# Sparse attention: the softmax of the compressed branch moved from ahead of the attention units to beside the scores of the first three

## The chip, the cores and the metric

The kernel runs on one core of a Trainium2 chip. The metric is the time of one execution of the whole program in device microseconds (us); the time before is the median of three runs. The program is a whole two-block network for 512 tokens (mixer with two kinds of attention, feed-forward layers, a second mixer, 32 experts); the change touches a stretch of some 30 us in the first mixer.

## The reference, cut to what matters

The sparse attention has three branches that share the queries: one over 31 compressed keys, one over selected blocks and one over a window. Each has a softmax of its own, and three gates weigh the results:

```python
s_c = jnp.einsum('btgrd,bjgd->bgrtj', q, k_cmp, ...) * scale
s_c = s_c - slopes[:, :, None, None] * dist_c
p_cmp = _masked_softmax(s_c, dist_c >= 0)
o_cmp = jnp.einsum('bgrtj,bjgd->btgrd', p_cmp.astype(v_cmp.dtype), v_cmp)
...
o = g[:, :, 0] * o_cmp + g[:, :, 1] * o_sel + g[:, :, 2] * o_win
```

With 512 tokens the 16 selected blocks and the window both hold every earlier token, so the second and third branch are full causal attention with a distance penalty. There are 8 heads in 2 groups; a head has 64 columns.

## The kernel before, in words

The stage is the function `nsa`. Its work has three parts.

**The compressed branch.** For each of the two groups, eight matmuls (L2111) give the scores of four heads against the compressed keys, transposed, in a PSUM tile of tag `sc`; ScalarE copies it to SBUF as `scT` (L2113). Then a loop over the four blocks of 128 tokens does the softmax: TensorE transposes the block of both groups back (L2119, two transposes, into `sc`), VectorE adds the mask (L2123), takes the maximum (L2124), subtracts it (L2125), multiplies by the slopes (L2126), ScalarE takes the exponential (L2127), VectorE sums (L2128), inverts (L2130), applies the gate (L2131, L2133) and scales (L2134), TensorE transposes the result `ec` (L2137, into a PSUM tile `pt`), ScalarE copies the high part to `PcTH` (L2138) and VectorE subtracts for the low part `PcTL` (L198, a helper's line). `PcT` is used first by the matmuls L2153 at the end of unit 1.

**The units.** `attend` runs 16 units, two branches for each of 8 heads. `att_scores` makes the scores of a unit in four row blocks of 128, 256, 384 and 512 keys (two matmuls L1973 each, of at least 256 columns, into `sc`); VectorE adds the penalty and takes the row maximum as it moves them to SBUF as `E` (L1975), and negates the maxima (`nm`, L1979). One step later `att_exp` takes the exponentials on ScalarE (L1987), inverts the sums (L1989), applies the gate (L1991) and scales `E` (L1996 on GpSimd and VectorE, L1994 on ScalarE). Another step later `att_av` transposes `E` (L2044), splits it into a high and a low part (L2050 on ScalarE, L198 on VectorE) and multiplies it with the values (L2053). So a unit is spread over three steps.

**The fill.** The matmuls of eight gate panels (L386, L389, tile `gm`) need nothing of this stage. `drip` hands them out in pieces of two, behind scores, transposes and output matmuls, at fixed rates (`FA`).

PSUM gives the tag `sc` two places; the compressed scores, their transposes and the scores of the units share them. The tag `pt` has three places. Before the change the tile `scT` lies in two of the three places of the tag `E3`, the 512-key block of a unit.

What each engine does next is an order that the framework fixes when the program is built: it takes instructions by the place where they are written, by what they depend on and by an internal estimate of times. An engine works off its list in that order, and a row that waits holds up all rows behind it. Weights come through SyncE's DMA queue, one panel of 512 KB at a time.

Of the kernel before, what the change touches and what calls it, by code (L numbers as in the profile page):

```python
# [8 lines left out]
F32 = mybir.dt.float32  # L9
# [7 lines left out]
T, D, P = 512, 1024, 128  # L17
NT = T // P
# [148 lines left out]
class Net:  # L167
# [1886 lines left out]
                          stop=u["last"] and j == NT - 1 and x is L, skip_group_check=True)  # L2054
            self.drip(last, self.rate)

    def attend(self, units, sp, pp, rate, lag=2):

        n = len(units)
        self.att_pad(sp)  # L2060
        self.rate = rate
        for t in range(n + lag):
            if t < n:
                u = units[t]
                if u.get("pre"):
                    u["pre"](u)
                self.att_scores(u, sp, pp)
            if 0 <= t - 1 < n:
                self.att_exp(units[t - 1], sp)
            if t >= lag:  # L2070
                u = units[t - lag]
                self.att_av(u, sp, pp)
                if u.get("post"):
                    u["post"](u)
        while self.pieces_:
            self.pieces_.pop(0)()
# [20 lines left out]
    def nsa(self, qst, KS, Vst, PcT, vcs, kcmp, gt, tb, oN, fill):  # L2097
        tc, V, S, PE = self.tc, self.V, self.S, self.PE
        with ExitStack() as st:
            sp = st.enter_context(tc.tile_pool(name="spn", bufs=1, reuse_waits="tile"))  # L2100
            self.at = st.enter_context(tc.tile_pool(name="spns", bufs=1, reuse_waits="tile"))
            pp = st.enter_context(tc.tile_pool(name="ppn", bufs=1, space=PSUM, reuse_waits="tile"))

            self.fill_start(fill, pp)
            tabc = tb["tabc"].rearrange("p (i j) -> p i j", i=NT)
            scT = []
            for g in range(2):
                ps = pp.tile([P, T], F32, name="sc", tag="sc", bufs=2)
                for x in range(2):
                    for j in range(4):  # L2110
                        last = PE.matmul(ps, lhsT=kcmp[x][:, g, 96 - 32 * j:224 - 32 * j], rhs=qst[:, 4 * g + j, :], start=x + j == 0, stop=x == 1 and j == 3)  # L2111
                scT.append(sp.tile([P, T], F32, name="scT", tag="E3", bufs=3))
                self.act = S.activation(scT[g], ps, AF.Copy)  # L2113
                self.drip(last, self.FA[1])
            for i in range(NT):
                tk = slice(i * P, (i + 1) * P)
                ps = pp.tile([P, 8, 32], F32, name="sc", tag="sc", bufs=2)
                for g in range(2):
                    last = PE.transpose(ps[:, 4 * g:4 * g + 4, :].rearrange("p a b -> p (a b)"), scT[g][:, tk], self.ident)  # L2119
                self.drip(last, self.FA[3])  # L2120
                e = sp.tile([P, 8, 32], F32, name="ec", tag="ec", bufs=2)
                m = self.at.tile([P, 8], F32, name="mc", tag="mc", bufs=2)
                V.tensor_tensor(e, ps, tabc[:, i, None, :].to_broadcast([P, 8, 32]), op=ALU.add)  # L2123
                V.tensor_reduce(m, e, axis=mybir.AxisListType.X, op=ALU.max)  # L2124
                V.tensor_tensor(e, e, m[:, :, None].to_broadcast([P, 8, 32]), op=ALU.subtract)  # L2125
                V.tensor_tensor(e, e, tb["slope"][:, :, None].to_broadcast([P, 8, 32]), op=ALU.mult)  # L2126
                S.activation(e, e, AF.Exp)  # L2127
                V.tensor_reduce(m, e, axis=mybir.AxisListType.X, op=ALU.add)  # L2128
                c = self.at.tile([P, 8], F32, name="ccc", tag="ccc", bufs=2)
                V.reciprocal(c, m)  # L2130
                V.tensor_tensor(c, c, gt[:, 0:8, i], op=ALU.mult)  # L2131
                if i == 0:
                    V.tensor_scalar(c, c, tb["valid"], None, op0=ALU.mult)  # L2133
                V.tensor_tensor(e, e, c[:, :, None].to_broadcast([P, 8, 32]), op=ALU.mult)  # L2134
                pt = pp.tile([P, 2, P], F32, name="pt", tag="pt", bufs=3)
                for g in range(2):
                    last = PE.transpose(pt[:, g, :], e[:, 4 * g:4 * g + 4, :].rearrange("p a b -> p (a b)"), self.ident)  # L2137
                self.act = S.activation(PcT[0][:, :, tk], pt, AF.Copy)  # L2138
                self.sub(PcT[1][:, :, tk], pt, PcT[0][:, :, tk])
                self.drip(last, self.FA[2])  # L2140
            units = []
            for h in range(8):
                g = h // 4
                cell = {}

                def newO(cell=cell):
                    cell["O"] = pp.tile([P, T], F32, name="O", tag="O", bufs=2)
                    return cell["O"]

                def post(u, h=h, g=g):  # L2150
                    r = slice((h % 4) * 32, (h % 4) * 32 + 32)
                    for x in range(2):
                        PE.matmul(u["O"], lhsT=vcs[r, g, :], rhs=PcT[x][r, g, :], start=False, stop=x == 1, skip_group_check=True)  # L2153
                    self.head_out(u["O"], oN, h, sp)

                for b in range(2):
                    units.append(dict(q=[qst[:, h, :]], k=KS[b][g], v=lambda j, b=b, g=g: Vst[:, j, 2 * b + g, :], tab=tb["tab"],
                                      scale=2.0 ** -(h + 1), gate=gt[:, 8 * (b + 1) + h, :], first=b == 0, last=False,
                                      O=None, newO=newO if b == 0 else (lambda cell=cell: cell["O"]), post=post if b else None))
            self.attend(units, sp, pp, self.FA[0])  # L2160


# [19 lines left out]
```

## Time and profile before

| | us |
|---|---|
| median of three runs | 1741.72 (1736.89 to 1745.83) |
| the profiled execution | 1744.53 |
| its span in the trace | 1742.7 |
| TensorE busy | 1636.6 (94%) |
| VectorE busy | 1246.2 (72%) |
| ScalarE busy | 934.2 (54%) |
| GpSimd busy | 380.8 (22%) |

The span is what the trace covers; 1.8 us of the profiled execution lie around it. The profiled execution is 2.8 us above the median. Busy shares are of the whole span, so the stretch of the change has to be read by itself: it lies from 92 us (first compressed scores) to 225.6 us (last output matmul of the stage).

### The profile page before, as it was taken

How to read it: one execution, taken by the hardware profiler on the slowest of the kernel's cores; microseconds unless marked ns; L12 is line 12 of the kernel's file. 1: busy time of each engine (PE TensorE's matmuls, PEld its weight loads, DVE VectorE, ACT ScalarE, POOL GpSimd, SP SyncE). 2: the span in 40 equal slices, each digit the busy share in tenths (PEclk: the TensorE clock that was granted, in tenths of full speed). 3: DMA queues.
4: the chain of work that ended last, by engine and by line, in shares of the span. 5: the costliest groups of instructions: out<-in, count | busy, mean ns of one | idle time of the engine just before them, and what ended most of it. 6: DMA issues, size and time to landing. Idle time of an engine off the chain costs nothing.

```text
span 1742.7 us, 24957 instructions
## 1 busy us (share of the span) xinstructions
PE 1636.6 (94%) x8980; PEld 1381.0 (79%) x8980; DVE 1246.2 (72%) x2281; ACT 934.2 (54%) x1588; POOL 380.8 (22%) x243
## 2 busy tenths in 40 slices
PE   8989999999999999999999999969999999989993
PEld 8868787877888888788769878758888788878882
DVE  5767857757787666533787875687888878897786
ACT  3457845664254444322554333346676667766763
POOL 3323401314144442000373221120100000101001
PEclk9989999999999999999999997969999999999997
DMA  5401213216333333322323212559999999999983
GB/s 153 108 25 38 43 55 68 60 37 226 128 109 97 97 97 97 114 92 70 116 84 98 79 43 67 208 176 340 381 387 402 374 400 406 405 363 402 391 345 109
DMA packets 214862, 317.55 MB, mean 182 GB/s; under 512 B 41997, under 2 KB 142524, under 8 KB 214735
## 3 DMA queue, kind: packets, MB, share of 16 engines
q1 hardware_dynamic: 209263, 303.91, 49.9%
q0 software_dynamic: 5472, 12.01, 1.9%
q8 instruction: 72, 1.18, 0.3%
q14 instruction: 55, 0.45, 0.1%
HBM read 308.06 MB, written 15.73 MB: 186 GB/s over the span
## 4 chain that ended last, share of the span: by engine, by line
PE 57%; DVE 8%; ACT 4%; DMA 3%; issue 3%; POOL 1%; DVEq 0%; SPq 0%; ACTq 0%; POOLq 0%
PE pA L205 13%; PE gate L1656 9%; PE pA L208 6%; PE up L1668 5%; PE dn L1702 5%; PE pA L810 4%; PE pA L809 4%; PE pA L811 4%; PE pA L958 2%; DVE wl L198 2%; ACT wh L1624 1%; DVE xL L198 1%; DMA raw<-in_w_up 1%; DMA raw<-in_w_down 1%; PE pB L278 1%
## 5 line engine op out<-in xcount | busy, mean ns | idle before, releaser
L198 DVE TENSOR_TENSOR wl<-wr,wh 128x1024 fp32r<-128x1024 f32 (+5 forms) x185 | 219.2, 1187 | 155.1 <-ACT wh L244 97.7
L241 POOL TENSOR_TENSOR wr<-wr,cols 128x1024 f32<-128x1024 f32 (+2 forms) x91 | 196.4, 2162 | 368.3 <-DMA wr<-in_w_in 135.4
L244 ACT ACTIVATE wh<-wr 128x1024 fp32r<-128x1024 f32 (+3 forms) x163 | 158.9, 980 | 193.0 <-PE pA L205 75.2
L1656 PEld LDWEIGHTS gate<-Xf,raw 128*128 128x128 f32 x2048 | 248.8, 191 | 11.2 <-ACT sil L1660 0.4
L198 DVE TENSOR_TENSOR wl<-raw,wh 128x1024 fp32r<-128x1024 f32 x172 | 207.0, 1227 | 54.3 <-ACT wh L1624 52.7
L1656 PE MATMUL gate<-Xf,raw 128*128 128x64 f32 x2048 | 243.3, 271 | 0.0
L205 PE MATMUL pA<-xL,wh 128*128 128x512 f32 (+1 forms) x544 | 193.6, 365 | 0.0
L205 PE MATMUL pA<-xH,wh 128*128 128x512 f32 (+1 forms) x544 | 193.3, 365 | 0.0
L1624 ACT ACTIVATE wh<-raw 128x1024 fp32r<-128x1024 f32 x172 | 175.1, 1051 | 12.2 <-PE dn L1702 6.5
L208 PE MATMUL pA<-xH,wl 128*128 128x512 f32 (+1 forms) x544 | 121.9, 365 | 0.0
L198 DVE TENSOR_TENSOR xL<-raw,xL 128x1024 fp32r<-128x1024 f32 x84 | 101.6, 1221 | 21.8 <-ACT xL L1624 20.5
L205 PEld LDWEIGHTS pA<-xL,wh 128*128 128x128 f32 x544 | 102.7, 189 | 16.7 <-issue 0.4
L205 PEld LDWEIGHTS pA<-xH,wh 128*128 128x128 f32 x544 | 102.5, 189 | 16.8 <-issue 0.4
L208 PEld LDWEIGHTS pA<-xH,wl 128*128 128x128 f32 x544 | 94.3, 189 | 16.0
L1624 ACT ACTIVATE xL<-raw 128x1024 fp32r<-128x1024 f32 x84 | 86.9, 1052 | 8.9 <-PE pC L1391 5.2
L1480 POOL DMA_INDIRECT Xr<-hnD,ix x16 | 23.7, 1482 | 248.9 <-issue 145.5
L1829 POOL DMA_INDIRECT yD<-yp,ix x14 | 23.4, 1673 | 212.7 <-DVE yp L1715 192.8
L810 PE MATMUL pA<-wh,actL 128*128 128x512 f32 x176 | 68.7, 390 | 0.0
L809 PE MATMUL pA<-wh,actH 128*128 128x512 f32 x176 | 68.5, 390 | 0.0
L811 PE MATMUL pA<-wl,actH 128*128 128x512 f32 x176 | 67.8, 390 | 0.0
L1702 PE MATMUL dn<-wl,hst 128*128 128x512 f32 x172 | 60.3, 414 | 3.9 <-DVE wl L198 3.2
L1996 POOL TENSOR_SCALAR E<-E,cc 128x128 f32<-128x128 f32 (+1 forms) x48 | 42.8, 901 | 91.1 <-DVE cc L1989 31.1
(691 smaller groups left out, 3799.8 us busy)
## 6 DMA issues: line engine op xcount, KB each, us to landing
raw<-in_w_gate SPq DMA_DIRECT2D x128, 512.0 KB
raw<-in_w_up SPq DMA_DIRECT2D x128, 512.0 KB
raw<-in_w_down SPq DMA_DIRECT2D x128, 512.0 KB
wr<-in_w_up SPq DMA_DIRECT2D x44, 512.0 KB
wr<-in_w_in SPq DMA_DIRECT2D x43, 512.0 KB
wr<-in_w_down SPq DMA_DIRECT2D x22, 512.0 KB
wr<-in_w_o SPq DMA_DIRECT2D x8, 512.0 KB
yD<-zero SPq DMA_DIRECT2D x8, 512.0 KB
```

The costliest lines, as they stand in the source:

```text
L198: return self.V.tensor_tensor(out, a, h.bitcast(F32), op=ALU.subtract)
L205: self.PE.matmul(ps, lhsT=ws(wh, k), rhs=xs(x, k), start=n == 0, stop=False)
L208: last = self.PE.matmul(ps, lhsT=ws(wl, k), rhs=xs(xh, k), start=False, stop=k == nk - 1)
L241: self.G.tensor_tensor(raw, raw, g[:, :, None].to_broadcast([P, nk, ncol]), op=ALU.mult)
L244: self.S.activation(H, raw, AF.Copy)
L809: self.PE.matmul(ps, lhsT=xs(0, a, i), rhs=H[:, k, :], start=a == 0, stop=False)
L810: self.PE.matmul(ps, lhsT=xs(1, a, i), rhs=H[:, k, :], start=False, stop=False)
L811: self.PE.matmul(ps, lhsT=xs(0, a, i), rhs=L[:, k, :], start=False, stop=a == nk - 1)
L1624: self.S.activation(H, raw, AF.Copy)
L1656: self.PE.matmul(ps[:, f, :], lhsT=raw[:, k, f * P:(f + 1) * P], rhs=u["Xf"](2 * p + k), start=p + k + f == 0, stop=p == 3 and k == 1, ski ...
L1668: self.PE.matmul(u[tag], lhsT=u["Xg"](2 * p + k), rhs=W[:, k, :], start=p + k == 0 and W is HL[0], stop=p == 3 and k == 1 and W is HL[1])
L1702: PE.matmul(u["dn"][hf], lhsT=u["hs"][:, p, :], rhs=W[:, 0, c], start=p == 0 and W is HL[0], stop=p == 3 and W is HL[1])
```

## The change

The body of the loop over the four blocks becomes a local function `compressed(i)`. `attend` gets a new argument, a table of functions for a step: after it has written the scores of unit t it calls the functions of step t. `nsa` hands it block 0 for step 0, blocks 1 and 2 for step 1 and block 3 for step 2. The tile `scT` gets a tag of its own with two places (4 KB more in each partition). Nothing is computed differently. In the changed file the lines of the block lie four further down (L2119 is L2123, L2137 is L2141).

```diff
-    def attend(self, units, sp, pp, rate, lag=2):
+    def attend(self, units, sp, pp, rate, beside={}, lag=2):
...
                 self.att_scores(u, sp, pp)
+            for f in beside.get(t, ()):
+                f()
             if 0 <= t - 1 < n:
                 self.att_exp(units[t - 1], sp)
...
-                scT.append(sp.tile([P, T], F32, name="scT", tag="E3", bufs=3))
+                scT.append(sp.tile([P, T], F32, name="scT", tag="scT", bufs=2))
...
-            for i in range(NT):
+
+            def compressed(i):
+
...
-            self.attend(units, sp, pp, self.FA[0])
+
+            self.attend(units, sp, pp, self.FA[0], {0: [lambda: compressed(0)], 1: [lambda: compressed(1), lambda: compressed(2)], 2: [lambda: compressed(3)]})
```

On TensorE, from the last gate pieces that go with the compressed scores, the order before has all eight transposes back and then the transposes of the first block's result:

```order
L386 MATMUL gm<-xL,wh 128x512
L2119 MATMUL sc<-ident,scT 128x128 x8
L2137 MATMUL pt<-ident,ec 128x128 x2
L386 MATMUL gm<-xH,wh 128x512
L386 MATMUL gm<-xL,wh 128x512
L2137 MATMUL pt<-ident,ec 128x128 x2
```

In the changed kernel the scores of unit 0 stand at that place, with two pairs of gate matmuls among them, and only then the first block's transposes:

```order
L1973 MATMUL sc<-KL_108,qst 128x256
L386 MATMUL gm<-xH,wh 128x512
L386 MATMUL gm<-xL,wh 128x512
L1973 MATMUL sc<-KH_107,qst 128x384
L1973 MATMUL sc<-KL_108,qst 128x384
L386 MATMUL gm<-xH,wh 128x512
L386 MATMUL gm<-xL,wh 128x512
L1973 MATMUL sc<-KH_107,qst 128x512
L1973 MATMUL sc<-KL_108,qst 128x512
L2123 MATMUL sc<-ident,scT 128x128 x2
```

The transposes back of the last block now follow the scores of unit 2. A little later on TensorE, in the changed kernel, the transposes of the third and fourth block's result stand like this, with the first scores of unit 3 ahead of them:

```order
L1973 MATMUL sc<-KL_112,qst 128x256
L2141 MATMUL pt<-ident,ec 128x128 x2
L386 MATMUL gm<-xH,wh 128x512
L386 MATMUL gm<-xL,wh 128x512
L386 MATMUL gm<-xH,wh 128x512
L386 MATMUL gm<-xL,wh 128x512
L386 MATMUL gm<-xH,wh 128x512
L386 MATMUL gm<-xL,wh 128x512
L386 MATMUL gm<-xH,wh 128x512
L386 MATMUL gm<-xL,wh 128x512
L2141 MATMUL pt<-ident,ec 128x128 x2
```

Eight gate matmuls have come between the two pairs of transposes; before, six L389 and the scores of unit 2 followed the fourth pair.

On VectorE the changed kernel's list of this stretch ends like this (PcTL is the last product of a block; the scores behind it are those of unit 3):

```order
L2134 RECIPROCAL ccc<-mc 128x8
L2135 TENSOR_TENSOR ccc<-ccc,gt 128x8
L198 TENSOR_TENSOR PcTL<-pt,PcTH 128x2x128
L2138 TENSOR_TENSOR ec<-ec,ccc 128x256
L198 TENSOR_TENSOR PcTL<-pt,PcTH 128x2x128
L1975 ISA E,mx<-sc,ta 128x128
L1975 ISA mx 128x1
L1975 ISA E,mx<-sc,ta 128x256
L1975 ISA mx 128x1
L198 TENSOR_TENSOR PTl<-pt,PTh 128x512
```

The scores of unit 3 stand behind the fourth block's PcTL; before, all of the four PcTL stood ahead of the last three scores of unit 2.

Because the order of the whole program comes out of one pass, other places change too, with the same instructions in another order. SyncE's queue of expert weights is one:

```order
-L1383 DMA hnD<-hnt 128x512 x4
-L1611 DMA raw<-in_w_down 128x1024
-L1383 DMA hnD<-hnt 128x512
+L1383 DMA hnD<-hnt 128x512 x5
+L1611 DMA raw<-in_w_down 128x1024
 L1611 DMA raw<-in_w_up 128x1024
 L1611 DMA raw<-in_w_gate 128x1024
```

Here one expert load moved behind a store; further down some 220 rows of loads stand in another order.

## Rows read from the trace of the kernel before

**Rows 1.** The page: span, busy time of TensorE, DMA share by slice.
```profile
span 1742.7 us, 24957 instructions
...
PE 1636.6 (94%) x8980; PEld 1381.0 (79%) x8980; DVE 1246.2 (72%) x2281; ACT 934.2 (54%) x1588; POOL 380.8 (22%) x243
...
DMA  5401213216333333322323212559999999999983
```

**Rows 2.** Busy time of each engine by stretch of the stage.
```profile
core 0: us, PE busy (x) PEld busy (x) DVE busy (x) ACT busy (x) POOL busy (x), PEclk, DMA share, GB/s
...
100.29:105.69 5.40, 0.00 (x1) 0.00 (x0) 5.19 (x14) 0.84 (x2) 2.15 (x1) 0.71 0.01 2
105.69:109.40 3.71, 3.67 (x12) 2.88 (x12) 2.87 (x10) 0.77 (x2) 0.00 (x0) 0.51 0.00 0
109.40:112.90 3.50, 2.35 (x8) 1.19 (x8) 3.50 (x18) 0.84 (x2) 0.00 (x0) 0.98 0.00 0
112.90:116.10 3.20, 3.19 (x10) 2.71 (x10) 1.77 (x10) 2.57 (x9) 0.00 (x0) 0.50 0.04 8
116.10:120.70 4.60, 3.29 (x18) 2.30 (x17) 4.60 (x16) 4.04 (x12) 2.87 (x2) 0.99 0.00 0
...
126.83:225.60 98.77, 96.28 (x543) 79.54 (x541) 77.73 (x230) 76.91 (x205) 34.92 (x34) 1.00 0.19 40
```

**Rows 3.** TensorE's waits from 92 to 230 us: total, times, longest.
```profile
PE pt L2137 <- DVE ec L2134: 5.4, 1, 5.4
PE sc L1973 <- DVE mx L1975: 1.9, 4, 0.7
...
PE pt L2044 <- POOL E L1996: 1.2, 1, 1.2
```

**Rows 4.** TensorE's timeline: start us, length us, engine, line, operation, [idle before <-releaser].
```profile
105.69 0.69 PE L2137 MATMUL pt<-ident,ec 128*128 128x128 f32 x2 [5.40 <-DVE ec L2134]
...
126.36 0.40 PE L386 MATMUL gm<-xH,wh 128*128 128x512 f32 x1
126.60 0.39 PE L386 MATMUL gm<-xL,wh 128*128 128x512 f32 x1
```

**Rows 5.** VectorE's timeline in the softmax of the first two blocks.
```profile
99.04 0.76 DVE L2123 TENSOR_TENSOR ec<-sc,ta 128x256 f32<-128x256 f32 x2 [1.90 <-PE sc L2119]
99.71 0.73 DVE L2124 TENSOR_REDUCE mc<-ec 128x8 f32<-128x256 f32 x2
...
101.03 2.45 DVE L2126 TENSOR_TENSOR ec<-ec,ta 128x256 f32<-128x256 f32 x2
...
104.31 0.32 DVE L2130 RECIPROCAL ccc<-mc 128x8 f32<-128x8 f32 x2
104.54 0.29 DVE L2131 TENSOR_TENSOR ccc<-ccc,gt 128x8 f32<-128x8 f32 x2
```

**Rows 6.** VectorE's timeline in the work of the units.
```profile
117.79 0.48 DVE L1996 TENSOR_SCALAR E<-E,cc 128x512 f32<-128x512 f32 x1
118.27 0.42 DVE L1975 CUSTOM_DVE_ANT_0 E<-sc,ta 128x256 f32<-128x256 f32 x1
...
118.62 1.22 DVE L198 TENSOR_TENSOR wl<-wr,wh 128x1024 fp32r<-128x1024 f32 x1
119.76 0.55 DVE L1975 CUSTOM_DVE_ANT_0 E<-sc,ta 128x384 f32<-128x384 f32 x1
...
120.23 0.69 DVE L1975 CUSTOM_DVE_ANT_0 E<-sc,ta 128x512 f32<-128x512 f32 x1
...
120.84 0.18 DVE L1989 RECIPROCAL cc<-sm 128x4 f32<-128x4 f32 x1
```

**Rows 7.** GpSimd's timeline at 101 us.
```profile
101.06 2.15 POOL L241 TENSOR_TENSOR wr<-wr,cols 128x1024 f32<-128x1024 f32 x1 [12.42 <-DMA wr<-in_w_in]
```

**Rows 8.** The expert stage: busy time as in rows 2, SyncE's longest wait.
```profile
1300.00:1400.00 100.00, 95.75 (x623) 81.59 (x621) 79.78 (x119) 67.83 (x101) 7.92 (x6) 1.00 1.00 391
...
SPq L1611 <- PE gate L1656: 127.9, 86, 4.6
```

## The prediction, as it was put on record

> **What bounds the kernel now.** I read the page first: TensorE is busy for 94% of the span, and the DMA engines are full only in the last third [rows 1]. So the time goes through TensorE up to the experts, and through DMA and TensorE together from there. Then I read the stage of the change in stretches [rows 2]. From 126.83 to 225.6 us TensorE is busy for 96.3 of 98.8 us: the steady run of the units is bounded by it, and no engine near it waits long. Ahead of that it is not. From 100.29 to 105.69 TensorE does nothing while VectorE is busy for 5.2 of 5.4 us: TensorE has made the transposes back of all four blocks' scores, and its next row, the transposes of the first block's result, waits for the scaling L2134 [rows 3, 4]. After that gap the granted clock is 0.51 for 3.7 us, the lower of the two levels (1.2 instead of 2.4 GHz); it rises, TensorE then waits for VectorE to empty the score tiles (four waits, 1.9 us) and the clock is at 0.50 again from 112.9 to 116.1 [rows 2, 3]. What is lost ahead of the steady run is thus 5.4 + 1.9 + 1.2 us of waits and half of 3.7 + 3.2 us at the low clock, 3.5 us: **12 us is the ceiling** of what this change can give back in its own stretch.
>
> The chain there is VectorE's. So the question is how much VectorE has to do until the steady run can start, and how long it waits itself.
>
> **The change part by part.** Nothing is removed or added: the same 8 + 8 transposes, 37 softmax operations on VectorE, 4 exponentials. They move to other places, and I follow one mark that both orders have: the pair of gate matmuls L386 behind the first two output matmuls of unit 0. Before, its second matmul starts at 126.60 [rows 4]. Up to the mark both orders have the same gate matmuls, the same scores of units 0 to 3, the same transposes; the order before also has two matmuls of unit 4, 256 columns each, together 0.23 us (half of the 0.24 us between two 512-column starts [rows 4], twice). What lies behind the mark is bounded by TensorE in both (the last line of [rows 2]), so what the mark wins is kept to the end of the stage, and all later work is moved by it.
>
> VectorE's list up to the mark, with times from start to start. A block of the softmax has seven passes over 256 columns, 0.335 us each (two L2123 from 99.04 to 99.71), and two small ones of about 0.12 us (two L2130 in 0.23) [rows 5]: 2.6 us, four blocks 10.4 us. A unit has four score passes, 0.35 us for 256, 0.47 for 384, 0.61 for 512 columns [rows 6], and 0.21 for 128 by the same step (an estimate from these three); with the scaling of E, 0.48, and three small ones, 0.4 in all, 2.5 us; three units 7.6 us. One split of a gate panel (wl) is 1.14 us [rows 6]. Together **19.1 us** from 99.0, when the first scores are there as the first transposes were: 118.1. Then two scores of unit 3 (0.56) and the first PTl (0.61, as 512 columns): 119.3, and TensorE needs one output matmul and one gate matmul more: the mark at 119.8. That is VectorE without a wait, 6.8 us earlier than now, 6.6 us net of unit 4's matmuls.
>
> It will wait in three places, as I find by going through the new order row by row with these durations. First, the scores of unit 0 go through two PSUM places by turns, each filled by TensorE only when VectorE has emptied it: 0.8 us until the first L2123 of the new order (VectorE's mask). Second, at the end: the third block's transposes wait for VectorE until about 116.9, and the fourth block's stand behind eight gate matmuls (8 x 0.23 = 1.84 us); VectorE finishes its other rows at about 118.8, and its next row, the last PcTL, can start at 119.9: 1.1 us, in which the scores of unit 3, long made, lie behind the waiting row. Third, the transposes of unit 0's E come only behind that pair, and its PTl 0.9 us later than VectorE could take it. So the mark comes at 119.8 + 2.8 = 122.6, 4.0 us earlier; **3.8 us net**.
>
> Two costs the trace of before bounds only. The clock: in my walk TensorE does about 0.8 us of work between 105.6 and 109.1, less than the 2.35 us busy of 109.4 to 112.9, behind which the clock was 0.50 [rows 2]; and it waits some 3.3 us from 113.7 to 117.0, behind which I expect what the 5.4 us gap brought. At the low clock the eight L389 and later the eight L386 take 1.8 us more each; of the first some 1.0 us reaches VectorE (it delays the 512-column scores of unit 2, which VectorE takes next), of the second all. Between 0 and 2.8 us; I take 2.0, since both patterns are nearer to rows that were followed by the low clock than to 116.1 to 120.7, which was not. The port: one L2126 of the first two took 2.1 us instead of 0.34 while GpSimd worked on a gate panel at 101.06 [rows 5, 7]. The panel comes at the same time, and in the new order VectorE reads PSUM in most of that time; between 0 and 1.7 us, I take 0.4, as one short SBUF pass can be caught.
>
> Sum: 3.8 - 2.0 - 0.4 = 1.4 us, between 6.6 and -0.9. The other parts cost nothing: scT in places of its own takes 4 KB of SBUF, and TensorE has no wait for the places that it leaves [rows 3]; ScalarE is busy for 9.1 of the 20.4 us from 100.29 to 120.70 now (the sum of five stretches, [rows 2]) and has room for the exponentials that come among those of the units; the gate panel that moved behind two scalings on GpSimd is used more than a unit later.
>
> Against the profiled execution of 1744.5 us this gives 1743.1; that execution lies 2.8 us above the median of the three, so against the median of 1741.7 it is **1740**.
>
> **A rule that speaks against the change.** In both kernels the scores go through two PSUM places, and the four waits of 1.9 us stood ahead of the second stretch at a clock of 0.50 [rows 2, 3]. The Trainium skill, page "TensorE: Matmul & The Clock Gate", section "A second HAM failure mode: psum-queue depth-cycling", says that a kernel which cycles through PSUM banks can leave TensorE idle so often and so shortly between groups of matmuls that its clock goes back and forth between the levels, and that the throughput is lost in the changes. The trace agrees for 109.4 to 116.1; by that rule the time is that of rival 2.
>
> **The rivals.** (1) VectorE hardly waits, and the clock stays up: the whole 6.6 us, 1735. For it: VectorE has always two kinds of work in its list. Against it: both waits at the end are in the order itself. (2) The clock goes back and forth through the whole stretch of scores: TensorE has scores, transposes and gate matmuls in small pieces from 99 to 122, and with half of some 24 us at the low level loses 6 us instead of 3.5 now. From 122.6 as the mark at full clock: 128.6, 2.0 us later than now, 1744. It decides if the stretch shows 0.5 for more than some 8 us (4.0 us won, at half a us for each). (3) Slower by over 0.5%: the order of expert loads on SyncE's queue has changed. In that stage a window of 100 us shows a DMA share of 1.00 with TensorE busy for 95.75 [rows 8]: no time to give. A load waits for its place (86 waits on the gate matmuls, 127.9 us in all, from 1200 to 1690 us), and all loads behind it wait too. With 490 us at that share, 2.2% of empty queue more cost 10.8 us: 1740 + 11 = 1751. It decides at 10 us; a drop of the share from 1.00 to 0.98 in all windows is the sign. Against it: the same loads in nearly the same turns, each still ahead of its use. (4) The other side of the same: the new order closes part of TensorE's 4.25 us of idle time in each 100 us there; half of it in 490 us would be 10 us, 1730. Against it: DMA is full already.
>
> That the change doesn't do what it says is excluded by the order: scores stand among the softmax on both engines.
>
> **How the numbers follow.** A measurement of this kernel can tell about 0.5%, 8.7 us, from no change. Forecast (1740) 0.47; rival 1 (1735) 0.18; rival 2 (1744) 0.11; rival 3 (1751) 0.12; rival 4 (1730) 0.12. Cases 0, 1 and 2 lie within 0.5% of 1741.7, 0.76 together, of which I leave 0.74, since rival 1 and a median at the lower end of the 9 us that the three runs spread can add up. Faster 0.14, slower 0.12. The range takes in both outer cases' near ends: 1729 to 1751.
>
> **What would show it right or wrong.** In the profile of the changed kernel: no wait of 5 us on L2134's successor at 100 us; VectorE busy almost throughout from 99 to 119; a gap of some 3 us on TensorE ahead of the third block's transposes, with a low clock behind it; the second gate matmul of the mark between 122 and 126; the last output matmul of the stage 1 to 5 us earlier than 225; from there to the end the same distances. It is wrong if the gap stays, if the mark is before 120, or if the stages after 230 us change by more than the mark does.

## The result, and the profile of the changed kernel

The changed kernel takes 1751.21 us (median of 20 executions; before 1742.11, also of 20): **1.0054 of the time before, 95% interval 1.0039 to 1.0069**. It is slower by half a per cent. The prediction was 1740, with a range that ended at 1751. The profiled execution took 1749.83 us with a span of 1748.0; the one of before 1744.53 and 1742.7 [rows 1].

**In the stage of the change** nearly everything came as predicted. The page of the changed kernel, as in [rows 1]:

```profile
span 1748.0 us, 24957 instructions
...
PE 1639.1 (94%) x8980; PEld 1381.0 (79%) x8980; DVE 1243.0 (71%) x2281; ACT 933.6 (53%) x1588; POOL 376.3 (22%) x243
```

Busy time by stretch, the columns of [rows 2]:

```profile
98.00:105.00 7.00, 4.72 (x22) 3.14 (x20) 6.28 (x23) 2.73 (x10) 1.90 (x1) 0.93 0.07 21
105.00:110.00 5.00, 3.58 (x11) 2.63 (x10) 4.50 (x19) 3.97 (x12) 3.44 (x4) 0.50 0.01 3
110.00:115.00 5.00, 3.81 (x18) 2.81 (x16) 4.98 (x18) 3.24 (x9) 0.00 (x0) 0.91 0.01 2
115.00:120.00 5.00, 3.31 (x12) 2.61 (x13) 3.65 (x13) 2.47 (x7) 2.12 (x3) 0.77 0.40 105
```

TensorE's waits from 92 to 230 us, as in [rows 3], and its timeline, as in [rows 4]:

```profile
PE sc L1973 <- DVE mx L1975: 3.6, 5, 1.0
PE pt L2141 <- DVE ec L2138: 2.9, 1, 2.9
PE O L2053 <- DVE PTl L198: 1.7, 3, 0.9
PE sc L2123 <- DVE mx L1975: 0.7, 2, 0.5
```

```profile
116.69 0.44 PE L2141 MATMUL pt<-ident,ec 128*128 128x128 f32 x2 [2.88 <-DVE ec L2138]
...
119.78 0.63 PE L2141 MATMUL pt<-ident,ec 128*128 128x128 f32 x2
...
123.69 0.39 PE L386 MATMUL gm<-xL,wh 128*128 128x512 f32 x1
```

The gap of 5.4 us on L2134 is gone. TensorE is busy for 4.7 of the 7 us from 98 to 105, where it stood still for most of the time before. The gap ahead of the third block's transposes is there, 2.88 us, and the clock is at the lower level from 105 to 110 and for a part of 115 to 120. The mark starts at 123.69 instead of 126.60. Of these 2.9 us 1.8 were there before the stage began: the last group of compressed scores started at 96.32 before and at 94.55 now. Counted from it the mark comes after 30.28 and 29.14 us, so the move won 1.1 us. To the end of the stage it keeps that: the last L2053 starts at 221.43 instead of 224.51, counted in the same way after 126.9 instead of 128.2 us. The expert stage then begins some 4 us earlier than before.

**In the expert stage** the time goes. It is measured here and below from the first row of the line of the gate matmuls, L1656, to the last gate matmul. That first row is a semaphore row in the queue of TensorE's weight loads; the first matmul itself comes 3.9 us behind it before and 3.3 us now. Before, then now:

```profile
L1656 PE MATMUL gate<-Xf,raw x2048: 217/275/323, 1180.0 to 1699.1; 128*128 128x64 f32 x187
L1656 PEldq EVENT_SEMAPHORE  x35: 51/51/51, 1176.1 to 1679.3; - x35
```

```profile
L1656 PE MATMUL gate<-Xf,raw x2048: 217/275/421, 1175.4 to 1704.5; 128*128 128x64 f32 x187
L1656 PEldq EVENT_SEMAPHORE  x35: 51/51/51, 1172.1 to 1684.7; - x35
```

This stretch takes 532.4 us instead of 523.0, and the whole loss is there: 4.0 us earlier at its start, 5.4 later at its end. (From the first matmul itself it is 529.1 instead of 519.1, a loss of 10.0.) One row for the stretch before, one for now, with the columns of [rows 2]:

```profile
1176.10:1699.10 523.00, 506.27 (x3330) 441.05 (x3329) 422.68 (x633) 362.90 (x530) 46.70 (x32) 1.00 0.99 383
```

```profile
1172.10:1704.50 532.40, 510.87 (x3331) 443.39 (x3329) 422.51 (x633) 362.45 (x530) 41.34 (x32) 0.99 0.98 376
```

The same number of matmuls; TensorE is busy for 4.6 us longer and idle for 4.8 us longer (21.5 instead of 16.7). The DMA share is lower by 0.01, where the third rival of the prediction had a drop of 0.02 as its sign, but the next rows speak against it as the cause. The first ones of TensorE's waits in this stretch (total, times, longest), before and now:

```profile
PE dn L1702 <- DVE wl L198: 3.2, 5, 1.2
PE dn L1702 <- DVE hst L198: 3.0, 4, 1.5
...
PE up L1668 <- ACT wh L1624: 1.2, 5, 0.4
PE gut L1679 <- ACT ups L1672: 0.7, 3, 0.2
...
PE dn L1702 <- ACT wh L1624: 0.7, 2, 0.4
```

```profile
PE up L1668 <- DVE wl L198: 3.8, 6, 1.3
PE dn L1702 <- ACT wh L1624: 2.9, 6, 1.2
PE gut L1679 <- ACT ups L1672: 2.8, 8, 0.7
...
PE up L1668 <- ACT wh L1624: 2.4, 5, 1.0
```

`wh` is the high part of a weight panel that ScalarE copies (L1624), `wl` the low part that VectorE makes from it, `ups` the up product on its way to the transposes. The waits that name ScalarE were 4.1 us in all and are 10.1; those that name VectorE went from 11.9 to 10.6. None names a load, nor does ScalarE wait for one in either kernel (VectorE once, for 0.5 us, before). SyncE's queue waits for places, as it did in [rows 8]:

```profile
SPq L1611 <- PE gate L1656: 142.7, 96, 4.6
```

So loads wait for engines here, not engines for loads. The longest of the waits on ScalarE shows how it comes about. TensorE, then ScalarE in the changed kernel, then ScalarE at the same place before:

```profile
1307.80 1.04 PE L1489 MATMUL tr<-ident,Xr 128*128 128x128 f32 x8
...
1309.14 1.89 PE L1656 MATMUL gate<-Xf,raw 128*128 128x64 f32 x16
1312.26 1.17 PE L1702 MATMUL dn<-wh,hst 128*128 128x512 f32 x2 [1.24 <-ACT wh L1624]
```

```profile
1308.43 1.69 ACT L1492 ACTIVATE xH<-tr 128x256 fp32r<-128x256 f32 x4
1310.18 1.08 ACT L1494 ACTIVATE Xf<-tr 128x512 f32<-128x512 f32 x2
1311.15 2.95 ACT L1624 ACTIVATE wh<-raw 128x1024 fp32r<-128x1024 f32 x3
```

```profile
1312.63 0.38 ACT L1492 ACTIVATE xH<-tr 128x256 fp32r<-128x256 f32 x1
1312.91 2.95 ACT L1624 ACTIVATE wh<-raw 128x1024 fp32r<-128x1024 f32 x3
1315.76 0.64 ACT L1492 ACTIVATE xH<-tr 128x256 fp32r<-128x256 f32 x2
```

Tokens are turned for each pair of experts (transposes L1489, copies L1492 and L1494). In the new order all six copies of one pair stand in a row ahead of three weight copies, 2.8 us, and TensorE has to wait for the first of them; before, one copy stood there. Right behind the wait the clock falls:

```profile
1300.00:1312.00 12.00, 10.79 (x74) 9.47 (x73) 9.29 (x20) 7.14 (x12) 1.02 (x1) 1.00 1.02 406
1312.00:1316.00 4.00, 3.74 (x12) 2.86 (x13) 3.76 (x5) 3.98 (x7) 0.00 (x0) 0.57 0.93 335
```

By the trace's clock records it is at the lower level for 3.4 us from 1312.4 and for 3.4 us from 1626.4, there behind a wait of 1.04 us on a weight copy of the same line. In the kernel before it does not fall in the whole stretch. The Trainium skill, page "TensorE: Matmul & The Clock Gate", section "A second HAM failure mode: psum-queue depth-cycling", says that a kernel that cycles through PSUM banks leaves TensorE idle for short times between groups of matmuls, often enough for its clock to go back and forth. The trace agrees that a short idle time can stand ahead of a fall, and not that it must come often: the two waits, of 1.24 and 1.04 us, lie 312 us apart.

### The profile page after: what moved, and what is told of

The parts are those of the page before. It is cut to its first block, busy times and chain, and to the rows that moved or that the text cites. A ratio compares the mean times of both kernels' runs of the same rounds, so it can differ in the third digit from the quotient of the medians.

```text
span 1748.0 us, 24957 instructions
## 1 busy us (share of the span) xinstructions
PE 1639.1 (94%) x8980; PEld 1381.0 (79%) x8980; DVE 1243.0 (71%) x2281; ACT 933.6 (53%) x1588; POOL 376.3 (22%) x243
## 4 chain that ended last, share of the span: by engine, by line
PE 57%; DVE 7%; ACT 4%; DMA 2%; issue 2%; POOL 2%; SPq 0%; DVEq 0%; ACTq 0%; POOLq 0%
PE pA L205 13%; PE gate L1656 10%; PE pA L208 6%; PE up L1668 5%; PE dn L1702 5%; PE pA L810 3%; PE pA L811 3%; PE pA L809 3%; PE pA L958 2%; DVE wl L198 2%; ACT wh L1624 1%; PE gut L1679 1%; PE pB L278 1%; DMA raw<-in_w_gate 1%; DVE xL L198 1%
## 5 line engine op out<-in xcount | busy, mean ns | idle before, releaser
L1656 PEld LDWEIGHTS gate<-Xf,raw 128*128 128x128 f32 x2048 | 249.5, 192 | 11.4 <-ACT sil L1660 0.4
L1656 PE MATMUL gate<-Xf,raw 128*128 128x64 f32 x2048 | 243.9, 272 | 0.0
L1624 ACT ACTIVATE wh<-raw 128x1024 fp32r<-128x1024 f32 x172 | 175.2, 1051 | 12.5 <-PE dn L1702 6.7
L205 PEld LDWEIGHTS pA<-xH,wh 128*128 128x128 f32 x544 | 102.2, 189 | 16.8 <-issue 0.4
L1624 ACT ACTIVATE xL<-raw 128x1024 fp32r<-128x1024 f32 x84 | 86.8, 1051 | 7.1 <-PE dn L1702 5.1
L1480 POOL DMA_INDIRECT Xr<-hnD,ix x16 | 19.4, 1215 | 252.4 <-issue 109.8
L1702 PE MATMUL dn<-wh,hst 128*128 128x512 f32 x172 | 60.3, 413 | 3.7 <-ACT wh L1624 2.9
```

The source lines that it names most:

```text
L205: self.PE.matmul(ps, lhsT=ws(wh, k), rhs=xs(x, k), start=n == 0, stop=False)
L1624: self.S.activation(H, raw, AF.Copy)
L1656: self.PE.matmul(ps[:, f, :], lhsT=raw[:, k, f * P:(f + 1) * P], rhs=u["Xf"](2 * p + k), start=p + k + f == 0, stop=p == 3 and k == 1, ski ...
L1702: PE.matmul(u["dn"][hf], lhsT=u["hs"][:, p, :], rhs=W[:, 0, c], start=p == 0 and W is HL[0], stop=p == 3 and W is HL[1])
```

## The experiments

**Theories.** A: the pass that orders the whole program put the expert stage in another order too, and that order costs the time; A1: by waits on ScalarE's and VectorE's copies and the clock that falls behind them; A2: by the order of the loads on SyncE's queue. B: the moved softmax itself. C: the places in SBUF, which all move with `scT`.

The table has, for each run, the stretch of the expert stage as measured above, TensorE's busy and idle time in it (the rows above, taken for each), the time at the lower clock in it (clock records) and the ratio to the time before. All but the ratio are of one profiled execution. The low clock is counted from the first gate matmul on; up to 3.1 us at the start of the stretch, left from a fall ahead of it, are not in it (1.7 us before, 0.3 in the changed kernel). What the texts below, recorded before each run, call the stretch from first to last gate matmul is this one.

| run | softmax | order of the expert stage | stretch us | busy | idle | low clock | ratio (95%) |
|---|---|---|---|---|---|---|---|
| before | ahead | before | 523.0 | 506.3 | 16.7 | 0 | 1 |
| E1 | beside | before | 523.6 | 506.9 | 16.7 | 0 | 0.9995 (0.9967 to 1.0022) |
| E3 | ahead | before | 523.6 | 506.8 | 16.8 | 0 | 0.9993 (0.9969 to 1.0016) |
| changed | beside | new | 532.4 | 510.9 | 21.5 | 6.8 | 1.0054 (1.0039 to 1.0069) |
| E4 = changed | beside | new | 532.4 | 510.8 | 21.6 | 6.8 | 1.0068 (1.0035 to 1.0102) |
| E2 | ahead | new | 543.1 | 521.3 | 21.8 | 27.3 | 1.0095 (1.0059 to 1.0131) |
| E5 | beside | new, split | 543.1 | 522.4 | 20.7 | 30.7 | 1.0036 (1.0009 to 1.0063) |
| E10 = E5 | beside | new, split | 530.6 | 508.7 | 21.9 | 0 | one execution |
| E6 | ahead | new, split | 530.6 | 508.7 | 21.9 | 0 | 1.0058 (1.0032 to 1.0085) |
| E7 | beside | third | 543.9 | 521.5 | 22.4 | 27.3 | one execution |
| E8 | ahead | third | 537.7 | 515.2 | 22.5 | 13.7 | one execution |
| E9 | beside | split everywhere | 535.3 | 510.1 | 25.2 | 6.8 | 1.0083 (1.0057 to 1.0109) |
| E11 | beside | both halves split | 579.7 | 522.0 | 57.7 | 68.3 | one execution |

**E1: the move, with the old order behind it.**

```diff
-            self.attend(units, sp, pp, self.FA[0], {0: [lambda: compressed(0)], 1: [lambda: compressed(1), lambda: compressed(2)], 2: [lambda: compressed(3)]})
+            self.attend(units, sp, pp, self.FA[0], {0: [lambda: compressed(0), lambda: compressed(1)], 1: [lambda: compressed(2), lambda: compressed(3)]})
```

> The softmax of the compressed branch stands beside the scores again, but with blocks 0 and 1 at unit 0 and blocks 2 and 3 at unit 1. On all engines the order behind this stage is then that of the kernel before, row for row; scT has places of its own as in the changed kernel. Theory A (the order of the expert stage costs the time): the stage of the change ends 1 to 4 us earlier than before, the expert stage takes the 523 us from its first to its last gate matmul that it took before (532 in the changed kernel) and 1.395 us a load (1.42 in the changed kernel), and the whole is 0.998 to 1.000 of the time before. Theory B (the moved softmax itself, or what it leaves behind in the next stages): 1.004 to 1.007. Theory C (the places in SBUF, that all move with scT): 1.004 to 1.007 too.

Measured: stretch 523.6, ratio 0.9995. The first output matmul of unit 0 comes 27.0 us after the last group of compressed scores, where it took 29.3 before (28.4 in the changed kernel), so this placing wins 2.3 us in its stage. B and C fall; 2.3 of 1742 us is 0.13%, and the interval can't show it.

**E2: the old place, with the new order behind it.**

```diff
-    FA = (0.7, 3, 1, 0)
+    FA = (0.7, 3, 0, 0)
```

> The softmax stands ahead of the units as before and scT lies in E3; only the number of gate matmuls behind each block's transposes is 0 instead of 1 (the third number of FA). Behind the stage the order of SyncE, ScalarE and VectorE in the expert stage is then that of the changed kernel, row for row, and TensorE's but for three small transposes. Theory A: slower as the changed kernel was, by 5 to 12 us (1.003 to 1.007), 1.41 to 1.43 us a load, the expert stage 529 to 535 us. Theories B and C: as before within 2 us (0.999 to 1.001), 1.395 us a load, apart from up to 2 us in the stage itself, whose order is also changed a little.

Measured: ratio 1.0095, stretch 543.1. Slower without any move of the softmax, and by more than expected: idle time is that of the changed kernel (21.8), but the clock is low for 27.3 us. These are the rows behind the same wait:

```profile
1315.00:1320.00 5.00, 4.79 (x19) 4.28 (x19) 4.97 (x7) 4.97 (x9) 0.00 (x0) 0.53 0.89 305
1320.00:1325.00 5.00, 5.00 (x20) 4.42 (x19) 4.97 (x7) 2.64 (x3) 1.86 (x1) 0.50 0.95 310
1325.00:1330.00 5.00, 5.00 (x23) 4.81 (x23) 0.65 (x1) 0.00 (x0) 0.00 (x0) 0.50 0.69 221
1330.00:1335.00 5.00, 5.00 (x15) 4.13 (x15) 0.00 (x0) 0.00 (x0) 0.00 (x0) 0.50 0.75 277
```

They also show which way the DMA share is tied: TensorE is fully busy at half speed, the other engines run out of work, and only then does the share go from 0.95 to 0.69, while SyncE's queue waits for places of the gate matmuls (10.9 us of the 16 from 1320 to 1336).

**E3: scT in places of its own, nothing else.**

```diff
-                scT.append(sp.tile([P, T], F32, name="scT", tag="E3", bufs=3))
+                scT.append(sp.tile([P, T], F32, name="scT", tag="scT", bufs=2))
```

> The kernel before with one edit: scT has places of its own, the softmax stands ahead of the units. The order is that of before on every engine; only addresses in SBUF differ. Theory A and B: 1.000. Theory C: 1.004 to 1.007.

Measured 0.9993 and 523.6: C falls. The other half alone, the move with `scT` left in E3, wasn't tried.

**E4: the changed kernel again.**

> The changed kernel itself, on the same chip as the three others, as their measure: 1.004 to 1.007 by the result, and a second look at which steps of the expert stage are slow. If slow stretches of loads come at the same loads as in its first trace, they belong to this order or to these weights; if at others, they are chance and only their sum belongs to the order.

Measured 1.0068, and the stretch repeats to a tenth: 532.4, with the same two falls of 3.4 us. That the clock falls at these two places belongs to this order, not to chance; for how long it falls doesn't, as E2 shows, where the expert stage has the same order but for three small transposes.

**E5 and E6: one cluster of copies taken apart,** in the changed kernel and in E2's.

```diff
-        self.S.activation(H, raw, AF.Copy)
+        self.lastw = self.S.activation(H, raw, AF.Copy)
...
-                self.turn(Xr[pr % 2], Xg[pr % 2], Xf[pr], 2, h)
+                with self.tc.issue_after(self.lastw.ins) if (pr, h) == (5, 1) else nullcontext(): self.turn(Xr[pr % 2], Xg[pr % 2], Xf[pr], 2, h)
```

> The changed kernel with one order constraint more: for the sixth pair of experts ScalarE's three copies of the second half of the turned tokens (two L1492, one L1494) may only come behind the weight copies L1624 that were written before them. On ScalarE the six copies that stood in a row there become three and three, VectorE's four passes two and two, TensorE's rows move at one place a little later; SyncE's order is the same, row for row. In the changed kernel TensorE waits 1.24 us for L1624 behind these six copies (at 1312 us) and has its clock at the lower level for 3.4 us right behind. Theory A1 (the order of the copies on ScalarE makes the wait, the wait brings the clock down): the wait is gone or under 0.5 us, the clock stays up there, and the stretch from the first to the last gate matmul is 2 to 4 us shorter than the 532.4 of the changed kernel. Theory A2 (the order of the expert loads on SyncE's queue, as the prediction's third rival has it): 532 as before. In either case the whole is too near to the changed kernel for the clock of the chip: 1.002 to 1.006 of the time before.

> The same constraint in the kernel with the softmax in its old place and the new order behind it (FA with 0 as third number), where the same wait of 1.23 us is followed by 20.5 us at the lower clock and the stretch from first to last gate matmul is 543.1 us. SyncE's order is again the same, row for row. Theory A1: the 20.5 us at the lower clock go (10 us) and the wait with them (1.2): 530 to 533 us, and the whole is 1.002 to 1.005 of the time before instead of 1.0095. Theory A2: 543 and 1.0095 still.

Measured in E6: 530.6 us instead of 543.1, no fall of the clock, ratio 1.0058 instead of 1.0095. TensorE at that place in E2, then in E6:

```profile
1314.39 0.73 PE L1702 MATMUL dn<-wh,hst 128*128 128x512 f32 x2 [1.23 <-ACT wh L1624]
...
1317.21 3.51 PE L1656 MATMUL gate<-Xf,raw 128*128 128x64 f32 x16
```

```profile
1312.48 0.73 PE L1702 MATMUL dn<-wh,hst 128*128 128x512 f32 x2 [0.75 <-ACT wh L1624]
...
1314.65 2.00 PE L1656 MATMUL gate<-Xf,raw 128*128 128x64 f32 x16
```

SyncE's order of loads is the same in both, and 12.5 us are gone, about half of the 27.3 us at the low clock: these are not the order of the loads, so for this part A2 falls. The ratio stayed above the 1.002 to 1.005 expected. In E5 the profiled execution, the longest of ten (1765.2 us, median 1749.8), had the wait at 0.75 us as well, and yet the clock fell for 20.5 us behind it: here A1 as expected, a shorter wait and no fall, failed.

**E10: the same kernel as E5 once more.**

> The changed kernel with the split copies of the sixth pair a second time. Its first profile had the wait at 0.75 us instead of 1.24 and still 20.5 us at the lower clock behind it, where the same split in the other kernel had 0.75 us and no fall. If the wait decides alone, this profile shows the fall again, 20.5 us; if the fall is a matter of the single execution at a wait of that size, it may show none, and the stretch from first to last gate matmul is then 527 to 529 us.

Measured: no fall, neither here nor behind the wait of 1.04 us later, which is still there; 530.6 us (527 to 529 expected). So with 0.75 us the fall is a matter of the single execution. The split took away the fall in two of three profiles, and not the other waits: idle time stays at 21.9.

**E7 and E8: a third order,** with the softmax beside the scores (FA `(0.7, 2, 1, 0)` in the changed kernel) and ahead of them (`(0.6, 3, 1, 0)` in the kernel before).

> The changed kernel with 2 instead of 3 gate matmuls behind the compressed scores (second number of FA): a third order behind the stage, the same on all engines as that of the next kernel. Theory A: the stretch from first to last gate matmul is the same in both within 1 us, whatever the place of the softmax; since the six copies stand in a row in this order too, there is a wait of over 1 us and a fall of the clock at that place, and the stretch lies between 527 and 545 us. Theory B (the place of the softmax): this one over 529, the next one at 523.

> The kernel before with 0.6 instead of 0.7 as the first number of FA: the softmax ahead of the units, the order behind the stage that of the kernel above on all engines. Theory A: its stretch from first to last gate matmul within 1 us. Theory B: 523 us as in the kernel before.

Measured 543.9 and 537.7: B falls again, since the kernel with the old place is far from 523. The expected 1 us was missed. The idle time is the same (22.4 and 22.5); the difference of 6.2 us is the clock, which fell at the same two places for 27.3 us in the one and 13.7 in the other, and half of 13.6 us is 6.8.

**E9 and E11: the split for all pairs,** on E1's kernel, with `pr and h` and with `pr` as the condition.

> The kernel of the first experiment (softmax beside the scores, order of before behind it) with the constraint of the split copies for all pairs of experts but the first: ScalarE's copies of the second half of the turned tokens come only behind the weight copies written before them, so that six of them never stand in a row ahead of a weight copy. The whole order of the expert stage changes with it. Theory A1: TensorE's waits on ScalarE's copies (L1624) fall below the 3.2 us that they have in the kernel before, the clock stays up, and the stretch from first to last gate matmul is 518 to 525 us (523.5 without the constraint); the whole is 0.995 to 1.001 of the time before. Against it: an order that is new in every pair can make other waits; then 525 to 532 and 1.001 to 1.005, with the waits on another tile.

> As the split for all pairs, but for both halves of the turned tokens: all six copies of a pair come behind the weight copies written before them. Theory A1: no wait on L1624 over 1 us behind the turned tokens, no fall of the clock; 518 to 528 us, the bound of the order's other waits.

Measured 535.3 us (ratio 1.0083) and 579.7 us (1800.5 us for the one execution), both above what was expected. The waits of E9, then of E11:

```profile
PE up L1668 <- ACT wh L1624: 4.6, 5, 1.1
PE dn L1702 <- DVE hst L198: 3.8, 1, 3.8
PE gate L1656 <- ACT Xf L1494: 2.7, 5, 1.4
```

```profile
PE up L1668 <- DVE xH L198: 23.3, 10, 5.2
PE dn L1702 <- ACT wh L1624: 16.8, 6, 4.9
```

A1's hope failed: taking the clusters apart everywhere made new waits, now for the turned tokens themselves. What it does show is the size of the lever: nearly the same set of instructions (16 of some 3300 on TensorE lie outside the stretch in E9 and E11) takes from 523 to 580 us here by its order, with what the clock does in it. No version was found that beats both kernels; E1 equals the kernel before.

**What follows for the cause.** The stretch is about 506 to 509 us of busy time at full clock, plus the idle time that the order brings, plus about half of the time at the low clock (E11 apart, where the busy time less half of the low clock is only 488 us). For the changed kernel: idle 4.8 us, clock 3.4 us, together 8.2 of the 9.4. That the order behind the stage is the cause is shown by E1, E2, E7 and E8. That the clock falls because of the wait behind the cluster of copies is not shown: it fell in all five profiles with the wait of 1.24 us and in neither E6 nor E10, but E5 had it with the cluster split, and longer waits elsewhere had none (last section). That the 4.8 us of idle time come from ScalarE's copies is read from the waits alone; no run puts back the order of the loads by itself, so A2 isn't excluded for them. The last 1.2 us (1.8 from the first matmul), busy time that grew with the order without a lower clock, stay open. So does why the clock stays low for 3.4 us in one execution and for 20.5 in another behind the same wait.

## Why the prediction was wrong

- **The move itself: right.** Gain 1.1 us, or 0.9 less the 0.23 us of unit 4's matmuls, against 1.4; the gap of 2.88 us against "some 3 us" and a low clock behind it; the mark at 123.69, between 122 and 126, though 1.8 of the 2.9 us by which it is earlier are owed to this execution's earlier start. The other low clock was forecast behind 105.6 to 109.1 and began at 104.0. The lower end of the sum is added wrongly: 3.8 - 2.8 - 1.7 is -0.7, not -0.9; the forecast doesn't use it.
- **"What the mark wins is kept to the end of the stage, and all later work is moved by it": the step that failed.** The first half holds. The second takes it that later stages run the same list; but the list of the expert stage was another one, and its stretch took 9.4 us more. The prediction named this as what would make it wrong.
- **Rival 3: the right place and, by luck, the right time, for a reason that the rows don't bear out.** It put the loss in the expert stage at 10.8 us and the time at 1751. Its mechanism is a load queue that is emptier and so holds up the work; but in the changed kernel no wait of TensorE, ScalarE or VectorE in the stage ends on a load, and in E2 the share falls where TensorE is slow. A share of 1.00 with a full queue was read as a bound in [rows 8]; the Trainium skill, page "Perfetto Trace Analysis", section "Identifying the Most-Contended Engine", warns that the occupancy of the DMA engines misleads, and the trace agrees: the share was 0.99 before, at 383 GB/s, and one wait of 0.5 us on VectorE was the only one in 523 us that ended on a weight load.
- **The chances.** Rivals 3 and 4 got 0.12 each, as if a new order were as likely to be better. The row to weigh was TensorE's idle time: 16.7 us of 523 before, so an order could win little and lose much. All the other orders run here lie above it (20.7 to 57.7). Seen from here 0.12 on the side that came true was little, and the range ended 0.2 us below the median.
- **The clock** was priced in the stage of the change, at 2.0 us, and not in the expert stage, where it cost about 3.4 of the 9.4 us. Rival 2 had as its sign 0.5 for more than some 8 us of the stage: the clock is low there for 10.2 us (6.8 from 104.0, 3.4 from 117.7), and the mark still won. Before it was low for 10.2 us too (from 102.5 and 112.8), so the sign could not tell the two apart.

## What to carry to other kernels

Where one pass orders a whole program, compare the order of every dense stage, not only of the stage that the edit touches, and price the difference there first: one per cent of a stage of 500 us is more than four times what the move won here. Read such a stage by TensorE's idle time and by who ends its waits; a full DMA queue was no bound here, where one wait of 0.5 us ended on a weight load. An edit is best judged with the later order held fixed, as in E1 here, since otherwise a small gain is measured together with a new draw of the order.

## What the runs showed of the hardware

- A single wait of 1.24 us, behind transposes and 64-column matmuls, was followed by the lower clock in all five profiles that had it at that place (3.4, 3.4, 6.8, 20.5 and 20.5 us, the waits 1.23 or 1.24). With 0.75 us it was followed by it in one of three (E5, E6, E10). The later wait of 1.04 us on the same copy was followed by it in the four profiles in which the clock had fallen at the first place too, and not in the two (E6, E10) in which it had not. So the length of a wait doesn't decide alone: the 1.54 us on `hst` that the kernel before has at 1232 us, also behind transposes and a few 64-column matmuls, stand in eleven of the thirteen profiles (all but E9 and E11) and were followed by it in none, and one of 1.34 to 1.38 us on `wl` in the eight profiles with the new or the third order was followed by it in one (E5, 3.4 us).
- Being busy doesn't bring the clock back at once: in E2 TensorE is busy without a pause for 15 us at 0.50, for the last 10 of them with ScalarE idle and VectorE busy for 0.65, and the clock came back only after 20.5.
- Up to the expert stage single executions differ by more than the move won: the first row of L1656 comes at 1162.2, 1176.1 and 1179.6 us in three kernels whose order behind the stage of the change is the same (E1, before, E3), and at 1172.1 and 1176.1 in two executions of the changed kernel. Within the expert stage the same order repeats to 0.6 us as long as the clock stays up.
